# HGRN scores for four heads at once in shared tiles, with three runs of level products and another order of gates, queries and values

## The chip, the cores and the metric

The kernel runs on one core of a Trainium2 chip. A core has a matrix engine (TensorE, PE in the profile, with its weight loads as PEld), three engines for elementwise work (VectorE or DVE, ScalarE or ACT, GpSimd or POOL) and a sequencer, SyncE or SP, that issues most of the DMA. They run side by side, each through its own queue in order, and wait for each other through semaphores. The metric is the time of one execution on the device in microseconds. Three executions of the kernel before took 1251.87, 1251.75 and 1250.62 us, so the median is 1251.75.

## What is computed

The program is a decoder of four layers over 256 tokens of width 1024. Each layer is a token mixer and a SwiGLU feed-forward block, each followed by a residual and a layer norm. The mixers are HGRN2, mLSTM, S5 and HGRN2 again. The change touches HGRN alone, which therefore runs twice, as the first and as the last layer. Per head (eight heads, 128 wide) its reference is this, by chunks, with `s_prev` the state that one chunk hands to the next:

```python
q, f, v, g = jnp.split(x @ w_in, 4, axis=-1)
log_f = jnp.logaddexp(jnp.log(lb), jnp.log1p(-lb) + jax.nn.log_sigmoid(f))
k = (1.0 - lb) * jax.nn.sigmoid(-f)
q = jax.nn.silu(q)
...
b = jnp.cumsum(lfb, axis=2)
diff = b[:, :, :, None, :] - b[:, :, None, :, :]
decay = jnp.exp(jnp.where(mask[:, :, None], diff, -jnp.inf))
att = jnp.einsum('bhtd,bhsd,bhtsd->bhts', qb, kb, decay)
o = jnp.einsum('bhts,bhse->bhte', att, vb) + jnp.einsum('bhtd,bhde->bhte', qb * jnp.exp(b), s_prev)
...
o = _head_rmsnorm(_from_chunks(oc), norm_w) * silu(g)
```

So the score of token t for an earlier token s is the sum over 128 channels of q, k and the product of the forget gates between them. In the first HGRN layer the bound `lb` is zero; in the last one it is not, and the gates then need two more instructions per head.

## The kernel before

**Projections.** A matrix of float32 is kept as a rounded part `hi` and a rest `lo`, and a product is three matmuls (`mm3`, lines 182 to 184). A weight stage of 1 MB comes by DMA (`fetch`, line 110, issued by SP, three staging buffers), is rounded by ACT (`halve`, line 151) and its rest is made by DVE (line 152), 1024 columns at a time. The list made by `plan` gives the order of stages, and `wstage` emits the splitting of the next stage when a stage is taken. Values and output gates are projected token by token, 512 columns wide, by `pieces`, four pieces of 12 matmuls for half the heads. Queries and forget gates are projected transposed, for two heads at a time, by `pair_proj`: 48 matmuls of 256 columns.

**Gates.** `hgrn_gates` makes k and f of two heads from one projection, with three ACT instructions, two on DVE and two on ACT (`act` is line 95), and in the last layer four bound instructions more. They need one activation table, the Silus of the queries another; `table` loads a table (line 88) and orders the activations around it.

**Scores.** A product of gates over a range of tokens can be split at any token in the range, so the scores are built by levels. At level m (1, 2, 4, ... 64) the tokens stand in pairs of neighbouring blocks of m; the query rows of the one block have been multiplied by the gates up to the block's edge, the key rows of the other by the gates from there, and one small product gives the scores between the two. `hgrn_scores` does this for a pair of heads, as a generator that yields after each level. It makes the diagonal products (line 654), masked by DVE into the tile `near` (line 655). For each level below 32, ACT copies the keys into `kk` (line 664), PE makes eight products of 32 by 32 (line 668), and DVE puts the valid ones into `near` by `copy_predicated` (line 671). Levels 32 and 64 are line 677, and their results go to the score tile `att` by ACT (line 684), the diagonal blocks by DVE (line 680). After the products of a level DVE multiplies keys, queries and the block's gate products in place (line 640), which the next level needs. The last step is the product between the two halves of the sequence (line 700), copied to `cross`.

**Order.** `scores` walks two pairs of heads level by level, and between the levels emits other work: the remaining query projections and the values during the first two pairs, the output gates during the last two. The framework places each engine's instructions by a list schedule in which earlier program order has priority and a ready instruction can fill a gap; the order is then fixed. `heads_out` makes the products with the values and the head norm, `turn` the gating and the transposes into `ot`, and `out_proj` the output projection. PSUM, where PE writes, has four banks with the tag `a` (scores, queries), two with `g` (projections) and two with `t`.

## Time and profile before

| what | value |
|---|---|
| median of three runs | 1251.75 us |
| the profiled execution: its time | 1251.88 us |
| the profiled execution: its span | 1250.1 us |
| mean granted clock of TensorE | 0.997 |

The page of the profile gives for each engine the time in which one of its instructions ran, as a share of the span. A matmul is pipelined: its duration overlaps with the next one's, and what it costs its neighbours is read from the distance of the starts in the timeline. The rows of the timeline are: start, duration, engine, line, operation, output and inputs, shapes, count. A row that stands for several merged instructions gives the time from the start of the first to the end of the last. In the groups by line the figures after the bar are the busy time in us and the mean duration of one in ns, then the idle time ahead of them.

### The profile page before, as it was taken

What the parts mean: (1) busy time and instruction counts of PE and PEld (TensorE: products, weight loads), DVE (VectorE), ACT (ScalarE), POOL (GpSimd) and SP (SyncE); (2) the same over time, 40 slices, a digit from 0 to 9 for tenths busy, and PEclk for the clock granted to TensorE, in tenths of its full rate; (3) what the DMA queues carried; (4) which work ended last, traced back from release to release, by engine and by line L of the source; (5) the groups of instructions that cost most, each with busy time, mean ns of one, the idle gap of its engine ahead of it and who ended that gap; (6) DMA issues with size and microseconds to landing.
All of it is one profiled execution on the core that took longest, in us unless ns stands there. A gap on an engine that the chain in (4) does not pass through costs nothing.

```text
span 1250.1 us, 21400 instructions
## 1 busy us (share of the span) xinstructions
PE 1230.6 (98%) x8464; PEld 1031.6 (83%) x8464; DVE 956.2 (76%) x1717; ACT 694.3 (56%) x1126; POOL 34.8 (3%) x63
## 2 busy tenths in 40 slices
PE   9999999999999999999999999999999999999997
PEld 8977888888798888888877788888889878888886
DVE  6887889796887799887699696666486887766664
ACT  7755575565477555555544355555359654555551
POOL 0000000000100000000000000000000000000000
PEclk9999999999999999999999999999999999999999
DMA  8733476666373288667565456555446432755540
GB/s 325 290 137 135 150 267 236 219 220 225 121 274 129 102 305 307 234 235 247 209 217 210 165 202 231 191 181 201 169 173 219 157 134 102 270 184 186 194 143 34
DMA packets 50245, 247.91 MB, mean 198 GB/s; under 512 B 6337, under 2 KB 15953, under 8 KB 23777
## 3 DMA queue, kind: packets, MB, share of 16 engines
q1 hardware_dynamic: 50016, 246.46, 55.0%
q8 instruction: 66, 1.08, 0.3%
q14 instruction: 35, 0.28, 0.1%
q0 software_dynamic: 128, 0.09, 0.0%
HBM read 233.94 MB, written 12.58 MB: 197 GB/s over the span
## 4 chain that ended last, share of the span: by engine, by line
PE 88%; DVE 6%; DMA 2%; ACT 2%; issue 1%; POOL 0%; SPq 0%; DVEq 0%; ACTq 0%; POOLq 0%
PE g L212 18%; PE g L182 10%; PE g L184 10%; PE g L183 9%; PE g L215 9%; PE a L183 8%; PE a L182 8%; PE a L184 8%; DVE lo L152 2%; PE a L374 1%; PE t L273 1%; DMA bc<-in_s_bc 1%; PE a L668 1%; DMA w<-in_w_gu 1%; PE a L548 1%
## 5 line engine op out<-in xcount | busy, mean ns | idle before, releaser
L152 DVE TENSOR_TENSOR lo<-w,hi 128x1024 fp32r<-128x1024 f32 x388 | 470.3, 1219 | 117.6 <-ACT hi L151 107.6
L151 ACT CAST hi<-w 128x1024 fp32r<-128x1024 f32 x388 | 405.3, 1051 | 186.5 <-PE a L183 98.0
L212 PE MATMUL g<-xx,hi 128*128 128x512 f32 x1024 | 356.6, 397 | 0.5 <-DVE sum L356 0.4
L215 PE MATMUL g<-xx,lo 128*128 128x256 f32 x1024 | 264.6, 279 | 0.0
L212 PEld LDWEIGHTS g<-xx,hi 128*128 128x128 f32 x1024 | 185.8, 188 | 37.5 <-DVE sum L356 1.2
L215 PEld LDWEIGHTS g<-xx,lo 128*128 128x128 f32 x1024 | 193.0, 188 | 10.8
L182 PE MATMUL g<-hi,xx 128*128 128x512 f32 (+1 forms) x416 | 166.5, 401 | 2.4 <-ACT xx L292 2.1
L184 PE MATMUL g<-lo,xx 128*128 128x512 f32 (+1 forms) x416 | 163.7, 395 | 0.0
L183 PE MATMUL g<-hi,xx 128*128 128x512 f32 (+1 forms) x416 | 163.4, 394 | 0.0
L183 PE MATMUL a<-hi,hl 128*128 128x512 f32 x328 | 129.3, 394 | 1.0 <-DVE hl L345 1.0
L182 PE MATMUL a<-hi,hh 128*128 128x512 f32 x328 | 129.0, 394 | 0.1
L184 PE MATMUL a<-lo,hh 128*128 128x512 f32 x328 | 129.0, 393 | 0.0
L355 ACT COPY sum<-g 128x256 f32<-128x256 f32 x128 | 47.7, 373 | 139.7 <-PE g L212 139.5
L356 DVE TENSOR_TENSOR sum<-g,sum 128x256 f32<-128x256 f32 x128 | 53.9, 421 | 61.9 <-ACT sum L355 61.5
L182 PEld LDWEIGHTS g<-hi,xx 128*128 128x128 f32 x416 | 78.4, 189 | 19.3 <-ACT xx L292 3.5
L184 PEld LDWEIGHTS g<-lo,xx 128*128 128x128 f32 x416 | 78.2, 188 | 16.4 <-DVE lo L152 0.4
L183 PEld LDWEIGHTS g<-hi,xx 128*128 128x128 f32 x416 | 78.4, 188 | 14.6
L183 PEld LDWEIGHTS a<-hi,hl 128*128 128x128 f32 x328 | 61.6, 188 | 15.6 <-DVE hl L345 1.8
L184 PEld LDWEIGHTS a<-lo,hh 128*128 128x128 f32 x328 | 61.6, 188 | 13.6
L182 PEld LDWEIGHTS a<-hi,hh 128*128 128x128 f32 x328 | 61.5, 188 | 13.3 <-ACT hh L344 0.9
L182 PE MATMUL g<-xx,hi 128*128 128x256 f32 x192 | 54.5, 284 | 0.0
L184 PE MATMUL g<-xx,hi 128*128 128x256 f32 x192 | 54.4, 283 | 0.0
(308 smaller groups left out, 1734.9 us busy)
## 6 DMA issues: line engine op xcount, KB each, us to landing
w<-in_w_gu SPq DMA_DIRECT2D x88, 1024.0 KB
w<-in_w_dn SPq DMA_DIRECT2D x44, 1024.0 KB
w<-in_w_hg SPq DMA_DIRECT2D x30, 1024.0 KB
w<-in_w_ml SPq DMA_DIRECT2D x12, 1024.0 KB
gb<-in_ln SPq DMA_DIRECT2D x8, 1024.0 KB
w<-in_w_ho SPq DMA_DIRECT2D x8, 1024.0 KB
w<-in_w_so SPq DMA_DIRECT2D x8, 1024.0 KB
w<-in_w_mo SPq DMA_DIRECT2D x4, 1024.0 KB
```

The costliest lines, as they stand in the source:

```text
L151: self.nc.scalar.copy(hi, x)
L152: i = self.nc.vector.tensor_tensor(lo, x, hi.bitcast(F32), ALU.subtract).ins
L182: mm(ps, lh, rh, start=start, stop=False)
L183: mm(ps, ll, rh, start=False, stop=False)
L184: mm(ps, lh, rl, start=False, stop=stop)
L212: whole = lambda: mm(ps, hi[:, c], self.xx[:, k].rearrange("p i t -> p (i t)"), start=k == 0, stop=k == KD - 1)
L215: mm(ps[:, S:], lo[:, c], self.xh[:, k], start=False, stop=False)
L273: nc.tensor.transpose(pt[:, (k % 4) * P : (k % 4 + 1) * P], z[:, k * P : (k + 1) * P], self.ident)
L355: nc.scalar.copy(t, ps[:, S:])
L356: nc.vector.tensor_tensor(t, ps[:, 0:S], t, ALU.add)
L374: nc.tensor.matmul(down[h][n], hidden(h, j, b)[x], dn[j][b][y][:, f], start=False, stop=(x, y, b) == steps[-1])
L548: nc.tensor.matmul(o, att[:, 2 * h + hd % 2, :], v[:, h, c], start=True, stop=h == 0)
```

## The change

Queries, keys and gates of four heads now lie in one tile each, 1024 columns wide (`part`), and one walk of `hgrn_scores` does four heads, so that there are two walks per layer instead of four. At each of the six levels below 64, ACT copies keys and queries, as they stand, into saved tiles (`levels`), and DVE multiplies them for the next level at once. The products are made later: levels 1, 2 and 4 in one run, 8 and 16 in another, 32 and 64 in the last (`RUNS`). `order` holds every product of a run behind the run's first, which is taken from the last of its levels, so that a run is ready as a whole when it begins. The copies of the diagonal blocks go from DVE to ACT.

The order of the projections changes with it: gates 0 and 1, queries 0 and 1, then, after the first six levels in the program, gates 2 and 3 and queries 2 and 3, each group behind a table load of its own, then the values. The mask tile is larger and is loaded after the first two gates. One score tile instead of three serves all heads, `near`, `ends` and `cross` have one buffer each, and the two halves of `ot` share buffers with the first two level tiles.

```diff
 MASKED = (1, 2, 4, 8, 16)
+NEAR = MASKED + (32,)
 BIG = 1e30
 AHEAD = 1
 ROWS = (0, 1, NBLK - 1)
 GAPS = (32, 256, 448)
+RUNS = ((1, 2, 4), (8, 16), (32, 64))
 
 
...
-            msk = hp.tile([P, len(MASKED) + 1, 64], F32, name=self.uid("msk"))
-            atts = [hp.tile([P, 512], F32, name=self.uid("att")) for _ in range(3)]
-            for t in atts:
-                nc.gpsimd.memset(t, 0.0)
-            ot = self.transposed(hp)
+            msk = hp.tile([P, len(MASKED) * P + 80], F32, name=self.uid("msk"))
+            att = hp.tile([P, 1024], F32, name=self.uid("att"))
+            nc.gpsimd.memset(att, 0.0)
             v = hp.tile([P, 2, D], F32, name=self.uid("v"))
             g = hp.tile([P, 2, D], F32, name=self.uid("g"))
 
...
+
+            def part(n, name, pr):
+                if (n, name) not in quads:
+                    quads[n, name] = wp.tile([P, 1024], F32, tag=name, name=self.uid(name))
+                return quads[n, name].rearrange("p (h x) -> p h x", h=2)[:, :, pr % 2 * 256 : pr % 2 * 256 + 256]
...
+                return self.hgrn_scores(hp, wp, *(quads[n, x] for x in "qkf"), msk, att)
+
+            def walk(n, run, times=1):
+                for _ in range(times):
+                    mem[n] = next(run)
 
             for halves in (both,) if j == 0 else ((0,), (1,)):
                 block(v, AF.Copy, 0, 0, halves)
-            self.table("natural_log_exp_and_others")
-            for pr in range(4):
-                gates(pr)
-            nc.sync.dma_start(msk, self.a["c_lvl"])
+            exp, silu = "natural_log_exp_and_others", "silu_and_others"
+            self.table(exp)
+            gates(0)
+            gates(1)
+            nc.sync.dma_start(msk[:, 0 : len(MASKED) * P + 32], self.a["c_lvl"])
             nc.sync.dma_start(nw, self.a["hg_nw"][j])
-            self.table("silu_and_others")
+            self.table(silu)
             query(0)
             query(1)
             v1 = pieces(v, AF.Copy, 0, 1)
             g0, g1 = (pieces(g, AF.Silu, 12, n) for n in range(2))
-            scores((0, 1), ([], [lambda: query(2)], [], [lambda: query(3)], v1[0:1], v1[1:2], v1[2:3], v1[3:]))
-            late = []
-            scores((2, 3), ([lambda: late.append(heads_out(0))], g0[0:1], g0[1:2] + [lambda: late.pop()()], g0[2:3], g0[3:], g1[0:1], g1[1:2], g1[2:3]))
+            first = scores(0)
+            walk(0, first, len(NEAR))
+            self.table(exp)
+            gates(2)
+            gates(3)
+            self.table(silu)
+            query(2)
+            walk(0, first)
+            query(3)
+            v1[0]()
+            walk(0, first)
+            v1[1]()
+            second = scores(1)
+            walk(1, second)
+            v1[2]()
+            walk(0, first)
+            walk(1, second, len(NEAR) - 1)
+            v1[3]()
+            walk(0, first)
+            g0[0]()
+            late = heads_out(0)
+            g0[1]()
+            g0[2]()
+            late()
+            g0[3]()
+            walk(1, second)
+            g1[0]()
+            g1[1]()
+            walk(1, second)
+            g1[2]()
+            walk(1, second)
+            g1[3]()
+            walk(1, second)
             gb = gb()
-            g1[3]()
+            ot = tuple(hp.tile([P, KD, S], F32R, tag="o", name=self.uid(n), bufs=2) for n in ("oh", "ol"))
             for h in range(2):
                 turn(0, h)
             heads_out(1)()
             self.out_proj(("w_ho", j), gb, ot, lambda h: turn(1, h))
...
+    def hgrn_gates(self, wp, pr, pf, lb, k, f):
 
         nc, act = self.nc, self.act
-        k, f = (wp.tile([P, 512], F32, tag=t, name=self.uid(t), bufs=4) for t in "kf")
         l = wp.tile([P, 512], F32, tag="t", name=self.uid("t"))
         act(l, pf, AF.Abs)
         act(l, l, AF.Exp, scale=-1.0)
         act(l, l, AF.Ln, bias=1.0)
+        pf, l = (x.rearrange("p (h x) -> p h x", h=2) for x in (pf, l))
...
+    def hgrn_scores(self, hp, wp, q, k, f, msk, att):
...
+        queries = lambda t, m: view(t, m, (512 - m, 2), (2 * m, 256 // m), (1, m))
+        whose = lambda e, m, s: view(e, s, (512 // m + 1 - 2 * s, 2), (2, 256 // m), (0, m))
+        eight = lambda x: x.rearrange("p (a t) -> p a t", a=8)
+        heads = lambda x: x.rearrange("p (a t) -> p a t", a=4)
         rows = lambda c: slice(32 * c, 32 * c + 32)
+        near = wp.tile([P, 256], F32, tag="near", name=self.uid("near"), bufs=1)
+        levels = [hp.tile([P, 2048], F32, tag="o", name=self.uid("lev"), bufs=2) for _ in range(2)]
+        levels.append(wp.tile([P, 2048], F32, tag="lev", name=self.uid("lev"), bufs=1))
+        saved = [t[:, i * 512 : (i + 1) * 512] for t in levels for i in range(4)]
+        k8, q8, a8 = eight(k), eight(q), eight(att)
+        pd = self.bank("a")[:, 0:256]
+        lead = None
+        for i in (2, 3, 6, 7, 0, 1, 4, 5):
             for c in range(4):
+                mm = nc.tensor.matmul(pd[rows(c), rows(i)], k8[:, i, rows(c)], q8[:, i, rows(c)], start=True, stop=True).ins
+                self.order(mm, lead)
+                lead = lead or mm
+        nc.vector.tensor_tensor(eight(near), eight(pd), msk[:, None, len(MASKED) * P : len(MASKED) * P + 32].broadcast_to([P, 8, 32]), ALU.mult)
         mul(q, q, f)
+        e, ends = f, wp.tile([P, 512], F32, tag="ends", name=self.uid("ends"), bufs=1)
         spare = 0
+        for g, m in enumerate(NEAR):
+            n = 512 // m
+            kc, qc = saved[2 * g : 2 * g + 2]
+            nc.scalar.copy(view(kc, 0, (m, 2), (2 * m, 256 // m), (1, m)), keys(k, m))
+            nc.scalar.copy(view(qc, 0, (256, 2), (m, 256 // m), (1, m)), queries(q, m))
+            for x, y in ((keys(k, m), 1), (queries(q, m), 0)):
+                mul(x, x, whose(e, m, y))
+            new = ends[:, 0:n]
+            if m > 1:
+                new, spare = f[:, spare : spare + n], spare + n
+            mul(new, e[:, 0::2], e[:, 1::2])
+            e = new
+            yield
+        for run in RUNS:
+            pl, lead = self.bank("a"), None
+            at = dict(zip(run, (pl[:, i * P :] for i in range(len(run)))))
+            for m in run[::-1]:
+                kc, qc = saved[2 * NEAR.index(m) : 2 * NEAR.index(m) + 2] if m < 64 else (k8, q8)
+                for a in range(4):
                     for c in range(4):
+                        o, x = at[m][rows(c)], kc
+                        if m < 32:
+                            o = o[:, 0:P].rearrange("p (h a t) -> p a h t", h=2, a=4)[:, a]
+                            x, y = kc[:, a * P + 32 * c :][:, 0:32], view(qc, (4 * a + c) * 16, (256, 2), (1, 16))
+                        elif m == 32:
+                            o = o[:, rows(a)]
+                            x, y = kc[:, a * P + 32 * c :][:, 0:32], qc[:, c % 2 * 256 + (2 * a + c // 2) * 32 :][:, 0:32]
+                        else:
+                            h = c // 2
+                            o = o[:, a * 64 : a * 64 + 64]
+                            x, y = k8[:, 4 * h + a, rows(c)], q8[:, 4 * h + a, 64 * (1 - h) : 64 * (2 - h)]
+                        mm = nc.tensor.matmul(o, x, y, start=True, stop=True).ins
+                        self.order(mm, lead)
+                        lead = lead or mm
+            for m in run:
+                if m < 32:
+                    three = lambda x: x.rearrange("p (h b m) -> p h b m", h=2, m=m)
+                    g = MASKED.index(m)
+                    nc.vector.copy_predicated(view(near, m, (P - m, 2), (2 * m, 64 // m), (1, m)), three(i32(msk[:, g * P : (g + 1) * P])), three(at[m][:, 0:P]))
+                    continue
+                for c in range(4) if m == 32 else ():
+                    nc.scalar.copy(a8[rows(c), :, rows(c)], eight(near[rows(c)]))
                 for s in range(0, P, m):
                     h = s // m % 2
                     t = s + m * (1 - 2 * h)
+                    nc.scalar.copy(a8[s : s + m, 4 * h : 4 * h + 4, t : t + m], heads(at[m][s : s + m, 0 : 4 * m]))
             if m < 64:
+                yield
+        for x, h in ((k8, 0), (q8, 4)):
+            x = x[:, h : h + 4, 0:64]
+            mul(x, x, e.rearrange("p (a s) -> p a s", s=2)[:, h : h + 4, 1:].broadcast_to([P, 4, 64]))
+        yield
         pc = self.bank("a")
+        for a in range(4):
+            nc.tensor.matmul(pc[:, a * P : (a + 1) * P], k8[:, a], q8[:, 4 + a], start=True, stop=True)
+        cross = wp.tile([P, 4, P], F32, tag="cross", name=self.uid("cross"), bufs=1)
+        nc.scalar.copy(cross, heads(pc))
+        yield a8, cross
...
-            p += [("w_hg", j, s) for s in (0, 1, 8, 9, 10, 11, 4, 5, 6, 7, 2, 3, 12, 13, 14, 15)] + [("w_ho", j, s) for s in range(4)]
+            p += [("w_hg", j, s) for s in (0, 1, 8, 9, 4, 5, 10, 11, 6, 7, 2, 3, 12, 13, 14, 15)] + [("w_ho", j, s) for s in range(4)]
...
-        lvl.append(np.concatenate([same & ((s // m) % 2 == h) for h in (0, 0, 1, 1)], 1))
-    lvl.append(s % 32 == np.arange(64)[None, :])
+        lvl += [same & ((s // m) % 2 == h) for h in (0, 1) for _ in range(4)]
+    lvl.append(s % 32 == np.arange(32)[None, :])
```

83 lines of the change are left out of this document (12 added, 71 removed).

## The prediction

> **What bounds the kernel.** I read the page first: the busy shares, then the chain that ended last. (On the page, PEld is TensorE's weight load.)
>
> ```profile
> span 1250.1 us, 21400 instructions
> ...
> PE 1230.6 (98%) x8464; PEld 1031.6 (83%) x8464; DVE 956.2 (76%) x1717; ACT 694.3 (56%) x1126; POOL 34.8 (3%) x63
> ...
> PE 88%; DVE 6%; DMA 2%; ACT 2%; issue 1%; POOL 0%; SPq 0%; DVEq 0%; ACTq 0%; POOLq 0%
> ```
>
> TensorE (PE) is busy 98% of the span and is 88% of the chain. Next, the busy time by stage of the two HGRN layers: the projections of gates and first queries, then the scores, for the first layer and for the last one.
>
> ```profile
> 16.70:51.40 34.70, 34.70 (x290) 34.55 (x288) 25.92 (x28) 30.26 (x42) 0.00 (x0) 1.00 0.86 316
> 51.40:108.00 56.60, 56.48 (x834) 44.80 (x834) 49.53 (x141) 32.57 (x68) 2.62 (x2) 1.00 0.37 133
> 933.20:970.30 37.10, 37.10 (x296) 36.13 (x294) 22.14 (x24) 33.44 (x55) 0.00 (x0) 1.00 0.65 243
> 970.30:1024.00 53.70, 53.55 (x821) 42.42 (x821) 49.85 (x142) 31.96 (x68) 2.19 (x2) 1.00 0.33 120
> ```
>
> The columns are the length, then busy PE, PEld, DVE (VectorE), ACT (ScalarE), POOL, clock, DMA share and GB/s. PE has no idle time worth naming in any of the four. So time can be won here only by making PE's own sequence shorter. Busy time does not say how well PE is fed, so I looked at start times in PE's timeline, around a run of small score products.
>
> ```profile
> 55.66 0.39 PE L183 MATMUL g<-hi,xx 128*128 128x512 f32 x1
> 55.98 0.46 PE L668 MATMUL a<-q,kk 128*32 128x32 f32 x32
> 56.37 0.50 PE L184 MATMUL g<-lo,xx 128*128 128x512 f32 x1
> 56.71 0.39 PE L182 MATMUL g<-hi,xx 128*128 128x512 f32 x1
> 56.94 0.40 PE L183 MATMUL g<-hi,xx 128*128 128x512 f32 x1
> ...
> 72.94 0.33 PE L677 MATMUL a<-q,k 128*32 128x32 f32 x16
> 73.21 0.51 PE L182 MATMUL g<-hi,xx 128*128 128x512 f32 x1
> 73.64 0.33 PE L677 MATMUL a<-q,k 128*32 128x32 f32 x16
> ...
> 103.25 0.39 PE L184 MATMUL g<-lo,xx 128*128 128x512 f32 x1
> 103.57 0.65 PE L677 MATMUL a<-q,k 128*32 128x64 f32 x32
> 104.15 0.50 PE L182 MATMUL g<-hi,xx 128*128 128x512 f32 x1
> 104.49 0.40 PE L183 MATMUL g<-hi,xx 128*128 128x512 f32 x1
> ```
>
> Undisturbed, a 512-wide projection product starts 0.23 us after the one before (56.71 to 56.94). From 55.66 to 56.71 PE did two of them and one run of 32 records (each product of this type is two records): 1.05 - 0.46 = 0.59 us for the run. From 72.94 to 73.64 it did a run of 16 and one projection product: 0.70 - 0.23 = 0.47. So 16 records cost 0.12 us, 7.5 ns each, and **0.35 us is the price of interrupting** the projections, whatever the run holds: the wide product before ends late, the one after starts late and slow. A run of 32 records 64 wide costs 1.24 - 0.46 = 0.78, so 13.4 ns a record over the same 0.35.
>
> **What the change takes from PE.** The first score run of each layer and the last of layer 3; the last of the first layer is the row at 103.57 above:
>
> ```profile
> 51.42 0.46 PE L654 MATMUL a<-q,k 128*32 128x32 f32 x32
> ...
> 970.32 0.46 PE L654 MATMUL a<-q,k 128*32 128x32 f32 x32
> ...
> 1019.63 0.65 PE L677 MATMUL a<-q,k 128*32 128x64 f32 x32
> ```
>
> Between them I count 23 interruptions by L654, L668 and L677 in each layer (two adjacent runs as one). The new code has four runs for four heads: the diagonal products, levels 1, 2 and 4, levels 8 and 16, levels 32 and 64. That is 8 per layer. The number of small products stays; here it is for the first layer:
>
> ```profile
> L668 PE MATMUL a<-q,kk 128*32 128x32 f32 x320 | 5.6, 200 | 0.0
> L677 PE MATMUL a<-q,k 128*32 128x64 f32 (+1 forms) x128 | 2.6, 212 | 0.1
> L654 PE MATMUL a<-q,k 128*32 128x32 f32 x128 | 1.9, 198 | 0.0
> ```
>
> By the code half of L677 is 32 wide, so 512 records at 7.5 ns and 64 at 13.4 ns, 4.7 us. Before: 23 x 0.35 + 4.7 = 12.75 us. After: 8 x 0.35 + 4.7 = 7.5. That is 5.25 us per layer; two of the 23 stand beside the products with the values and shared a switch with them, so I take **5.0 per layer, 10.0 in all**. The crosswise product (L700) keeps its records and loses one or two cheap switches of about 0.1 us: nothing.
>
> One price is not in these rows. The new runs hold 64 to 96 records of the narrow kind; the longest above is 48. S5 has a long run, of the wider kind:
>
> ```profile
> 644.48 1.99 PE L1206 MATMUL g<-s5u,bm 128*32 128x64 f32 x128
> 646.40 0.39 PE L183 MATMUL a<-hi,xx 128*128 128x256 f32 x1
> ```
>
> 128 records in 1.92 us is 15 ns each with the switch, the pace of the short 64-wide run, so length itself slows nothing there. Whether PE is fed at 7.5 ns for that long is open. If past 32 records the pace fell to 13.4 ns, 32 + 64 + 32 + 32 = 160 records per four heads would lose 5.9 ns each: 0.9 us, 3.8 in the kernel. The lower end is 0; I take 0, since the form of these records is that of the 7.5 ns rows.
>
> **What it does to the other engines.** Prices, in the first layer's HGRN stretch, then two rows of the last layer, then the table load and its neighbours, and the issue of the mask:
>
> ```profile
> L152 DVE TENSOR_TENSOR lo<-w,hi 128x1024 fp32r<-128x1024 f32 x34 | 40.7, 1219 | 10.7 <-ACT hi L151 10.7
> L151 ACT CAST hi<-w 128x1024 fp32r<-128x1024 f32 x33 | 34.2, 1045 | 13.9 <-PE g L183 9.8 <-PE a L184 4.0
> L640 DVE TENSOR_TENSOR q<-q,f 128x256 f32<-128x256 f32 x20 | 8.4, 418 | 0.0
> L95 ACT ACTIVATE t<-t 128x512 f32<-128x512 f32 x8 | 5.0, 629 | 0.0
> ...
> 952.57 0.59 ACT L95 ACTIVATE f<-f,odds 128x256 f32<-128x256 f32 x1
> 953.06 0.50 ACT L95 ACTIVATE k<-k,odds 128x256 f32<-128x256 f32 x1
> ...
> 45.07 0.64 ACT L95 ACTIVATE k<-k 128x512 f32<-128x512 f32 x1
> 45.72 1.28 ACT L88 ACT_TABLE_LOAD   x1
> 47.02 0.60 ACT L95 ACTIVATE q<-a 128x512 f32<-128x512 f32 x1
> ...
> msk<-in_c_lvl SPq DMA_DIRECT2D x2, 192.0 KB
> ```
>
> DVE gets lighter: for four heads two instructions 256 wide (2 x 0.42 us) become one 512 wide (about 0.68: the rows of 256 and 1024 elements lie 801 ns and 768 elements apart, 1.04 ns an element). For the 24 such pairs per layer that is 0.16 each, 4 us, and the copies of the diagonal go to ACT. ACT gets heavier: per four heads and level one 512-wide copy of keys and one of queries (0.63 each by L95) where there were two copies of keys, and two more table loads per layer, 2.6 us.
>
> The crowded place is new. Gates 2 and 3 and queries 2 and 3 now run on PE while the first six levels are multiplied. PE has four projections of 48 products there, at 34.70 / 290 = 0.12 us each: 23.0 us. ACT must do four weight splits (8 x 1.05), two gate pairs (10 x 0.63), twelve level copies (12 x 0.63), two table loads and three Silus (0.6 each): 26.6 us. The last layer adds eight bound instructions, 4 x 0.59 + 4 x 0.50 = 4.4, so 31.0. If nothing could be moved, PE would lack 3.6 and 8.0 us, 11.6 together. But much can move. In the two query projections before it, ACT has per projection of 5.8 us only a split and a Silu (2.7), so about 6 us of splits can be made ahead, as far as buffers allow; the last gate pair's exponentials and the Silus may run late, since the second four heads start only after 24 products of the values, 24 x 0.23 = 5.5 us later. The row 933.20:970.30 shows how this ends: ACT 90% busy and PE still without a gap. The bounds are 0 and 11.6.
>
> A second crowded place is the six levels of the second four heads, which must be done before PE has used up the rest of the values and the output gates. From their start to their last run PE has 24 + 48 + 36 projection products, 24.8 us, and some 7 us of runs and of products with the values. DVE needs there twelve level products (8.2), about 5 for the other instructions of the levels and for masks, ten splits (12.2) and 2.7 at the heads' output, 28 of 32 us. That share is the one of the row 51.40:108.00, 49.53 of 56.60, where PE did not wait; if it fails, PE stands idle late in the layer. For both places together I take 1.5 us, near the two rows without a gap.
>
> The Trainium skill speaks against the extra loads: "ScalarE: Activation LUTs", section "What ACT_TABLE_LOAD costs", puts a switch at about 2.66 us, 1.28 of load and 1.38 of drain, and asks to group by set. Here the load took 1.28 us, began where the activation at 45.07 ended and was followed 0.02 us later: the drain does not show. By the page's figure ACT would carry 5.5 us more over the kernel, an estimate, and the sum would stay as it is while ACT is off PE's path.
>
> Smaller edits, at nothing. The mask tile grows from 192 KB to 336 KB and its DMA moves ahead of gates 2 and 3 on SP's queue; the weight fetches behind it come 144 KB / 316 GB/s = 0.5 us later, three staging buffers ahead of use. The masked diagonal tile has one buffer, so the second four heads' diagonal product on DVE must wait for ACT's copies after the first four's last run, one piece of values (12 x 0.23 = 2.8 us) and the run of about 1 us later; behind it on DVE stand level products and a split, while PE has two pieces prepared, 5.5 us. The output halves share buffers with the level copies; they are needed some 10 us after the last reader.
>
> **Sum.** The profiled execution took 1251.9 us for its span of 1250.1; the median of the runs is 1251.75, 0.1 less. 1251.75 - 10.0 + 1.5 = **1243.2**.
>
> **Rivals.** (1) The work cannot be moved so far and PE waits 4 to 7 us in the crowded places of both layers: 1245.7 to 1248.7. For: 26.6 and 31.0 against 23.0. Against: the slack just named. Nothing measurable is left if the waits reach 7.5 to 12.5 us: about 1251. (2) **Slower**: the level copies and products, earlier in the program, sit ahead of the weight splits on ACT's and DVE's queues. A level alone is two copies and two products, 2 x 0.63 + 2 x 0.68 = 2.6 us if ACT and DVE alternate without overlap, 15.7 for six; one stage prepared ahead feeds PE for 5.8, so PE stands for 10 us per layer, 20 in all: 1262. It decides from 5 us per layer. For: the twelve copies and twelve products are one chain through both engines. Against, the queues of before in the first levels:
>
> ```profile
> 52.02 1.05 ACT L151 CAST hi<-w 128x1024 fp32r<-128x1024 f32 x1
> ...
> 53.10 1.23 DVE L152 TENSOR_TENSOR lo<-w,hi 128x1024 fp32r<-128x1024 f32 x1
> ```
>
> Splits were placed between the level steps. (3) It does not do what it says: projections slip into the runs, or long runs lose pace. Half the interruptions kept leaves 1247; the lost pace gives 1246.5. One page bears on the pace: "TensorE: Matmul & The Clock Gate" of the Trainium skill, in its table of figures, gives a queue 64 deep, less than a run of 96 with its weight loads. The S5 run, twice that, kept pace, so it has little weight.
>
> **Chances.** Forecast with PE waits under 4 us 56% (1241 to 1245.7), rival 1 as a gain 14%, rival 3 7%, waits that eat the gain 11%, slower 12%. The range of 1240.2 to 1250.5 leaves out rival 2, the upper part of the eaten gain, and below it a few per cent. 0.2% is 2.5 us, about what a measurement of this kernel tells from no change. Faster 0.77, same 0.11, slower 0.12.
>
> **What would show it.** Right: in each HGRN layer PE's timeline has eight runs of 64 or more small records instead of 23, a 96-record run with its switch takes about 1.07 us (0.35 + 96 x 7.5 ns), and the first projection product of query 3 starts no later than 23 us after that of gate 2 plus the runs between. Wrong: idle time before weight loads, released by L151 or L152, between gates 2 and the second block of values, or before the last runs of a layer; runs at 13 ns a record; or small runs split by projection products.

## The result and the profile after

The changed kernel took 1242.92 us (median; 1242.01 to 1243.72), the kernel before 1251.66 us beside it: a ratio of 0.9932, 95% interval 0.9917 to 0.9947. In a second comparison, further below, it took 1243.04 against 1250.28, ratio 0.9939 (0.9927 to 0.9951). The ratios compare executions at full clock: one of the five executions with the values by VectorE, in the experiments below, took 2006.62 us at a granted clock of 0.556 and is left out. The profiled execution took 1242.15 us. Its page has these lines in the place of those shown of before:

```profile
span 1240.4 us, 21170 instructions
...
PE 1220.3 (98%) x8464; PEld 1029.4 (83%) x8464; DVE 943.3 (76%) x1577; ACT 713.8 (58%) x1126; POOL 32.5 (3%) x59
...
PE 85%; ACT 6%; DVE 6%; DMA 2%; issue 1%; SPq 0%; DVEq 0%; POOL 0%; ACTq 0%
```

TensorE has the same 8464 matmul records and is as full as before, and its busy time fell by 10.3 us. To see where, cut both executions at the same four places: the first gate projection of each HGRN layer, and the last product with values of that layer. Here are busy times by stretch, before and then after (length first, then PE, PEld, DVE, ACT, POOL, clock, DMA share, GB/s): first HGRN layer, everything between the two, last HGRN layer.

```profile
16.78:116.85 100.07, 99.95 (x1177) 87.12 (x1176) 81.76 (x175) 68.34 (x119) 2.62 (x2) 1.00 0.57 208
116.85:933.22 816.37, 805.78 (x5013) 671.78 (x5012) 644.29 (x1151) 445.49 (x707) 23.89 (x45) 1.00 0.58 207
933.22:1032.91 99.69, 99.55 (x1171) 86.44 (x1170) 77.76 (x171) 70.97 (x131) 2.19 (x2) 1.00 0.48 177
```

```profile
17.38:113.37 95.99, 95.60 (x1177) 86.98 (x1176) 74.85 (x105) 77.60 (x119) 1.87 (x2) 1.00 0.59 217
113.37:927.24 813.87, 804.13 (x5012) 670.72 (x5011) 644.40 (x1151) 446.06 (x707) 23.26 (x43) 1.00 0.58 208
927.24:1023.17 95.93, 94.90 (x1172) 86.28 (x1170) 71.42 (x101) 80.61 (x131) 1.84 (x2) 1.00 0.51 181
```

The two HGRN layers are shorter by 4.08 and 3.76 us, 7.8 together. The spans differ by 9.7, because the stretch between the layers, which the change does not touch, was by chance 2.5 us shorter in this execution, while the start was 0.6 later. Most of the 2.5 is one place in S5. PE's timeline there, before and then after:

```profile
692.27 0.50 PE L183 MATMUL a<-hi,xx 128*128 128x512 f32 x1 [2.00 <-ACT xx L95]
...
693.00 0.63 PE L182 MATMUL a<-hi,xx 128*128 128x512 f32 x1
693.42 0.63 PE L183 MATMUL a<-hi,xx 128*128 128x512 f32 x1
```

```profile
688.90 0.50 PE L185 MATMUL a<-hi,xx 128*128 128x512 f32 x1 [2.08 <-ACT xx L97]
...
689.47 0.40 PE L184 MATMUL a<-hi,xx 128*128 128x512 f32 x1
689.70 0.40 PE L185 MATMUL a<-hi,xx 128*128 128x512 f32 x1
```

Both executions idle about 2 us there. In the one, products then start 0.43 us apart at a granted clock of 0.5; in the other 0.23 apart at 1.0. From the first of these rows to the next other work is 4.07 us in the one and 2.52 in the other, so 1.55 of the difference is this. A second profiled execution of the changed kernel had the dip again, and its span was 1242.9; its two layers were 7.2 us shorter than before. So the change itself is worth 7 to 8 us, 7.8 in the first execution. The ratios say 8.5 (0.0068 x 1251.66) and 7.6 (0.0061 x 1250.28), and the interval of each holds both layer figures.

Inside the layer, PE's timeline has the runs that the code asks for:

```profile
58.52 0.28 PE L186 MATMUL a<-xx,hi 128*128 128x256 f32 x1
58.73 1.03 PE L722 MATMUL a<-lev 128*32 128x32 f32 x96
59.69 0.39 PE L184 MATMUL a<-xx,hi 128*128 128x256 f32 x1
59.91 0.28 PE L185 MATMUL a<-xx,lo 128*128 128x256 f32 x1
...
68.39 0.76 PE L722 MATMUL a<-lev 128*32 128x32 f32 x64
69.08 0.50 PE L184 MATMUL g<-hi,xx 128*128 128x512 f32 x1
...
72.04 0.76 PE L684 MATMUL a<-q,k 128*32 128x32 f32 x64
75.66 0.65 PE L722 MATMUL a<-q,k 128*32 128x64 f32 x32
76.13 0.50 PE L722 MATMUL a<-lev 128*32 128x32 f32 x32
```

Two 256-wide products take 0.24 us when nothing is between them, so the run of 96 cost 59.91 - 58.52 - 0.24 = 1.15 us. By the sum of start distances over all eight runs and the products behind them, runs and switches together got some 4.8 us cheaper in each layer (from 12.9 and 13.1 to 8.2). 4.8 x 2 = 9.6, and 7.8 came out: some 1.8 us went into new waits and what came with them. The longest, in the last layer, on PE's timeline, and then ScalarE's (ACT) timeline at the same time:

```profile
988.63 1.05 PE L745 MATMUL a<-q,k 128*128 128x128 f32 x8
990.26 0.50 PE L184 MATMUL g<-hi,xx 128*128 128x512 f32 x1 [0.57 <-ACT v L527]
991.76 0.61 PE L548 MATMUL a<-v,att 128*128 128x128 f32 x4
992.73 0.50 PE L184 MATMUL g<-hi,xx 128*128 128x512 f32 x1 [0.37 <-ACT v L527]
```

```profile
986.48 1.89 ACT L736 COPY att<-a 32x128 f32<-32x128 f32 x6
988.39 0.67 ACT L695 COPY lev<-q 128x512 f32<-128x512 f32 x1
988.97 0.61 ACT L694 COPY lev<-k 128x512 f32<-128x512 f32 x1
989.61 0.60 ACT L527 ACTIVATE v<-g 128x512 f32<-128x512 f32 x1
```

The values are finished on PE when the crosswise product starts at 988.63, but ACT copies them out of PSUM at 989.61, behind score copies and level copies of the next four heads. PE needs the bank for the output gates and waits. The products with the values (L548) also fall into two pieces around this wait.

### The profile page after: what moved, and what is told of

Its sections match the earlier page's. It is cut to its first block, busy times and chain, and to the rows that moved or that the text cites. A ratio compares the mean times of both kernels' runs of the same rounds, so it can differ in the third digit from the quotient of the medians.

```text
span 1240.4 us, 21170 instructions
## 1 busy us (share of the span) xinstructions
PE 1220.3 (98%) x8464; PEld 1029.4 (83%) x8464; DVE 943.3 (76%) x1577; ACT 713.8 (58%) x1126; POOL 32.5 (3%) x59
## 4 chain that ended last, share of the span: by engine, by line
PE 85%; ACT 6%; DVE 6%; DMA 2%; issue 1%; SPq 0%; DVEq 0%; POOL 0%; ACTq 0%
PE g L214 18%; PE g L184 9%; PE g L217 9%; PE g L186 9%; PE g L185 9%; PE a L185 8%; PE a L186 8%; PE a L184 8%; ACT hi L153 2%; DVE lo L154 1%; PE a L376 1%; PE t L275 1%; DMA bc<-in_s_bc 1%; ACT L90 1%; DVE s5rot L1267 1%
## 5 line engine op out<-in xcount | busy, mean ns | idle before, releaser
L154 DVE TENSOR_TENSOR lo<-w,hi 128x1024 fp32r<-128x1024 f32 x388 | 470.8, 1220 | 119.5 <-ACT hi L153 110.7
L153 ACT CAST hi<-w 128x1024 fp32r<-128x1024 f32 x388 | 404.9, 1051 | 173.1 <-PE a L185 96.2
L217 PE MATMUL g<-xx,lo 128*128 128x256 f32 x1024 | 264.6, 279 | 0.0
L186 PE MATMUL g<-xx,hi 128*128 128x256 f32 x192 | 54.5, 284 | 0.0
L185 PE MATMUL g<-xx,lo 128*128 128x256 f32 x192 | 54.4, 283 | 0.0
```

Of the source, the lines that this page charges most:

```text
L153: self.nc.scalar.copy(hi, x)
L154: i = self.nc.vector.tensor_tensor(lo, x, hi.bitcast(F32), ALU.subtract).ins
L185: mm(ps, ll, rh, start=False, stop=False)
L186: mm(ps, lh, rl, start=False, stop=stop)
L217: mm(ps[:, S:], lo[:, c], self.xh[:, k], start=False, stop=False)
```

## The experiments

All of them are one edit of the changed kernel, except the one on order, which is an edit of the kernel before. The theory (A) is that of the prediction: PE's sequence is made of projections, narrow runs and a price per interruption. The stretch is the length of an HGRN layer, cut as above; the groups are the narrow runs per HGRN layer that PE's timeline shows.

| kernel | groups | stretch, first | stretch, last | ratio to before (95%) |
|---|---|---|---|---|
| before | 23 | 100.07 | 99.69 | 1 |
| order alone | 20 | 98.69 | 98.25 | 0.9975 (0.9963 to 0.9988) |
| seven runs | 14 | 97.67 | 97.26 | 0.9972 (0.9962 to 0.9982) |
| changed | 8 | 95.99 | 95.93 | 0.9932 (0.9917 to 0.9947) |
| changed, again | 8 | 95.97 | 96.56 | 0.9939 (0.9927 to 0.9951) |
| values by VectorE | 8 | 95.02 | 94.94 | 0.9922 (0.9909 to 0.9934) |
| values first | 8 | 95.46 | 95.31 | 0.9935 (0.9913 to 0.9958) |
| two runs | 6 | 98.76 | 99.34 | 1.0014 (1.0005 to 1.0022) |
| two runs, relieved | 6 | 96.46 | 96.04 | 0.9965 (0.9953 to 0.9978) |
| joined runs | 3 | 99.05 | 101.88 | 1.0008 (0.9997 to 1.0018) |

**Order alone.** The kernel before, two heads at a time, with gates 2 and 3 put between the first levels and the order of queries and values of the change:

```diff
-            for pr in range(4):
+            for pr in range(2):
                 gates(pr)
...
-            scores((0, 1), ([], [lambda: query(2)], [], [lambda: query(3)], v1[0:1], v1[1:2], v1[2:3], v1[3:]))
+            scores((0, 1), ([lambda: self.table(exp), lambda: gates(2)], [lambda: gates(3), lambda: self.table(silu)], [lambda: query(2)], [lambda: query(3)], v1[0:1], v1[1:2], v1[2:3], v1[3:]))
```

> The kernel before with the new order of projections alone: gates 0 and 1, queries 0 and 1, then gates 2 and 3 and queries 2 and 3 between the levels of the first two pairs, with the two further table loads; scores in pairs, level by level, as before. TensorE's program has 20 interruptions by small products in each HGRN layer instead of 23, since some of them now fall together. Theory A: 3 x 0.35 = 1.05 us less per layer, about 1249.6 us, up to 1252 if TensorE waits in the crowded place. Theory B (the order carries the gain): near 1243 us.

It took 1247.76 us, more of a gain than A had and far from B. The layers got 1.38 and 1.44 us shorter, where three interruptions fewer account for 1.05 each; what the other 0.35 is was not followed. So the order carries about a third of the change's 7.8, and, by the price of an interruption, most of that by having fewer of them.

**Seven runs.** Four heads at once as in the change, but one run per level, with a step of the walk after each projection or piece:

```diff
-RUNS = ((1, 2, 4), (8, 16), (32, 64))
+RUNS = ((1,), (2,), (4,), (8,), (16,), (32,), (64,))
...
             gates(2)
+            walk(0, first)
             gates(3)
+            walk(0, first)
...
```

> The changed kernel, with the six levels and level 64 sent as seven runs between products instead of three; tiles shared by four heads, saved copies and the order of projections stay. In each HGRN layer TensorE's program has 14 interruptions by small score products instead of 8. Theory A (an interruption costs 0.35 us, whatever it holds): 6 x 0.35 = 2.1 us more per layer, 4.2 in all, about 1247.1 us. Theory B (the gain came from lighter VectorE work, the saved copies and the new order, the number of runs does not matter): 1242.9 us, and HGRN stretches as long as in the changed kernel, 96.0 us.

1247.32 us: A. The layers are 1.68 and 1.33 us longer than in the changed kernel. Six interruptions at 0.35 would be 2.1. The trace shows what is lacking. Around one of the runs of 32 records PE starts its products at 69.51, 70.21 and 70.55 us, so the run costs 1.04 - 2 x 0.23 = 0.58; the run of 96 in the changed kernel cost 1.15. Three short runs in place of that one are 0.60 more, 0.30 for each further interruption, because the records of a short run go by faster (about 7 ns each, 8.4 in the runs of 64 and 96). In the last layer, PE also idles 0.60 us in all, against 0.95 in the changed kernel.

**More cuts.** The price itself, by adding interruptions: in the middle of each piece of the second values block and of the output gates stands one more narrow product, which nobody reads.

```diff
-                    self.as_part(dict(enumerate(ps)), [us[u]], 2 * u)
+                    self.as_part({0: ps[0]}, [us[u]], 2 * u)
...
+                    cut = nc.tensor.matmul(spare[0][0:32, 0:32], self.ident[:, 0:32], self.ident[:, 0:32], start=True, stop=True).ins
+                    self.order(cut, self.last)
+                    self.as_part({1: ps[1]}, [us[u]], 2 * u)
```

> The changed kernel with 12 more products per HGRN layer, each 32 rows by 32 columns of the identity, put singly between two 512-wide projection products in the middle of a piece of the values or output gates; their results are read by nobody. 24 more interruptions in all. A (each interruption of the projections costs 0.35 us, and about 8 ns per record): 24 x (0.35 + 0.02) = 8.8 us more, 1242.9 + 8.8 = 1251.7, and each HGRN layer's stretch 4.4 us longer than 96.0. B (what the change gained was the waits around the old order of work, and a single narrow product between two wide ones costs its own 8 to 25 ns): under 1 us, 1243 to 1244.

1250.82 us against 1250.02 for before: ratio 1.0002 (0.9992 to 1.0012). Twenty-four products of two records each eat the gain of the whole change. PE's timeline around one of them, then from the view of that one source line PE's idle time ahead of it (the sum, and how often):

```profile
66.86 0.39 PE L186 MATMUL g<-lo,xx 128*128 128x512 f32 x1
67.18 0.25 PE L526 MATMUL t<-ident 128*32 128x32 f32 x2
67.36 0.50 PE L184 MATMUL g<-hi,xx 128*128 128x512 f32 x1
67.69 0.39 PE L185 MATMUL g<-hi,xx 128*128 128x512 f32 x1
```

```profile
  issue: 8.6, 24
```

From 66.86 to 67.69 PE starts two wide products and the narrow one: 0.83 - 2 x 0.23 = 0.37 us. By the stretches, 4.12 and 4.33 us longer with 12 more products each, it is 0.34 and 0.36. The idle ahead of each is 8.6 / 24 = 0.36, and nothing that the profile shows ends it. This is A's number, and B (a single narrow product costs its own few nanoseconds) falls.

**Wide cuts.** The same, with the whole identity as the weights:

```diff
-                    cut = nc.tensor.matmul(spare[0][0:32, 0:32], self.ident[:, 0:32], self.ident[:, 0:32], start=True, stop=True).ins
+                    cut = nc.tensor.matmul(spare[0][:, 0:32], self.ident[:, :], self.ident[:, 0:32], start=True, stop=True).ins
```

> As the run with 24 more 32 by 32 products, but each added product uses all 128 rows and all 128 columns of the identity as its weights, with 32 moving columns, and writes all 128 partitions. A1 (the price is that of going from the whole array to a 32-column part of it and back): these cost no more than the crosswise products' switches did, about 0.1 us and 0.1 us for the records, so 24 x 0.1 to 0.2 = 2.4 to 4.8 us, 1245.3 to 1247.7. A2 (the price belongs to going from the products of halves to plain fp32 products, whatever the shape): as much as with the 32 by 32 products, 8.8 us, about 1251.7.

1247.45 us, ratio 0.9975 (0.9966 to 0.9985). PE's timeline:

```profile
66.30 0.39 PE L186 MATMUL g<-lo,xx 128*128 128x512 f32 x1
66.53 0.30 PE L526 MATMUL t<-ident 128*128 128x32 f32 x2
66.67 0.48 PE L184 MATMUL g<-hi,xx 128*128 128x512 f32 x1
66.98 0.40 PE L185 MATMUL g<-hi,xx 128*128 128x512 f32 x1
```

Now the cost is 66.98 - 66.30 - 0.46 = 0.22 us, 0.14 of it the two records, and the product starts on time, 0.23 after the one before. By the stretches it is (98.50 - 95.99) / 12 = 0.21. The time lies at the upper end of A1's range and far from A2: such a product costs a little more than A1 had, and the delay ahead of it is gone. That delay belongs to the 32-column form. "TensorEngine Tiling (Array Packing)" in the Trainium skill, section "Key Properties", says that a change of tiling mode drains TensorE; the rows agree, and put the price of going there and back at 0.37 us with one product in it.

**Two runs.** Levels 1 to 8 in one run of 128 records, 16 to 64 in one of 96:

```diff
-RUNS = ((1, 2, 4), (8, 16), (32, 64))
+RUNS = ((1, 2, 4, 8), (16, 32, 64))
...
             query(2)
-            walk(0, first)
             query(3)
...
             g1[1]()
-            walk(1, second)
             g1[2]()
```

> Levels 1, 2, 4 and 8 in one run of 128 records and 16, 32 and 64 in another of 96, each set of four heads with its diagonal apart as in the changed kernel, so 6 interruptions per HGRN layer instead of 8. A (price of an interruption 0.35 us, runs of up to 128 records hold no idle, since a block of TensorE's instructions is 128 records long and no run uses up two of them): 2 x 2 x 0.35 = 1.4 us less than the changed kernel, 1241.5 or a ratio of 0.992, HGRN stretches about 95.3. F2 (a run of 128 records already uses up its block before the next has landed): an idle of 0.5 to 3 us without a releaser in at least one run, 1243 to 1248. W (the levels' copies are late for the longer runs): idle of 1 us or more in the products around them with ScalarE or VectorE as releaser, 1242 to 1245.

1252.96 us, ratio 1.0014 (1.0005 to 1.0022): W, and worse than W gave. The runs hold no idle, the waits come behind them. PE's timeline in the first layer, then ACT's:

```profile
79.20 1.05 PE L743 MATMUL a<-q,k 128*128 128x128 f32 x8
81.86 1.35 PE L548 MATMUL a<-v,att 128*128 128x128 f32 x10 [1.60 <-issue]
```

```profile
78.57 1.68 ACT L730 COPY att<-near 32x256 f32<-32x256 f32 x4
80.27 1.88 ACT L734 COPY att<-a 32x128 f32<-32x128 f32 x6
```

PE is through with the crosswise products at 80.26 and starts the products with the values at 81.86, when the score copies (L734), which they read, are nearly through. The trace names no releaser for this wait; that it is these copies is read from the times. With all later levels in one run, all their copies come at once and last, on an engine that is full. The two layers are 6.2 us longer than in the changed kernel and what follows the last one is 1.3 longer; the rest of the 10 us lies in the layers between and was not followed.

**Joined runs.** As the two runs, but the runs moved until a run stands directly behind another and the second heads' diagonal behind that, so that there are only three groups per layer:

```diff
+            walk(0, first, 2)
             second = scores(1)
             walk(1, second)
...
-            walk(1, second)
             g1[0]()
             g1[1]()
-            walk(1, second)
+            walk(1, second, 2)
             g1[2]()
```

> The changed kernel with all seven levels of four heads sent in one go, from two banks of results, the first one joined to the diagonal products of the second four heads: 3 interruptions by small products in each HGRN layer instead of 8. Theory A: 5 x 0.35 = 1.75 us less per layer, 3.5 in all, about 1239.4 us, if nothing new has to be waited for; the last scores are one piece earlier than before, so the masks and copies behind them have 5.5 us of products to hide in. Theory B: no gain, 1243 us or more.

1251.86 us: no gain, as B had it, and 9 us lost besides, which neither theory gave. The gain of five interruptions is more than lost again, and by idle time inside the groups, for which the trace has no releaser. PE's timeline in the last layer, then busy time by stretch, then the DMA queues in the first two of these stretches (packets, MB, share):

```profile
985.22 0.56 PE L680 MATMUL a<-q,k 128*32 128x32 f32 x40
990.76 0.54 PE L680 MATMUL a<-q,k 128*32 128x32 f32 x22 [4.98 <-issue]
```

```profile
986.00:988.40 2.40, 0.00 (x0) 0.00 (x0) 1.89 (x7) 0.00 (x0) 0.00 (x0) 1.00 0.99 406
988.40:989.40 1.00, 0.00 (x0) 0.00 (x0) 0.00 (x0) 0.00 (x0) 0.00 (x0) 0.95 1.12 401
991.00:995.00 4.00, 4.00 (x30) 3.17 (x21) 3.20 (x6) 2.24 (x6) 0.00 (x0) 0.50 0.05 18
```

```profile
q1 hardware_dynamic: 131, 0.97, 99.0%
...
q1 hardware_dynamic: 51, 0.39, 105.7%
q8 instruction: 1, 0.02, 5.8%
```

PE stops in the middle of 64 like products; 42 of them are done, and from 987.92 on no engine does anything. Only the DMA engines are full, with weights, until at 988.4 one packet of another queue comes through: q8, instructions. PE goes on 1.4 us after it has landed, at half clock (0.50 in the last of the three stretches), which costs more.

The page says what q8 is. These are its rows of the changed kernel and, ahead of its description, of the long runs below:

```profile
q8 instruction: 66, 1.08, 0.3%
```

```profile
q8 instruction: 74, 1.21, 0.4%
```

8464 matmuls and as many weight loads, 16928 instructions, in 66 packets: 256 a packet. The long runs add 2 x 1024 instructions and have eight packets more, again 256 each. So q8 brings PE's instructions, 128 records with their loads at a time. At 8.4 ns a record a block is used up in 1.1 us; in projections it lasts 15 us or more. A new theory (F), then: a narrow run that uses up a whole block before the next has landed stops PE.

**Long runs and short runs.** To test F without data to wait for: 128 products of the identity (256 records) in a row, at two places of each HGRN layer; and the same products 32 at a time, in each of eight pieces.

```diff
+                    add, lead = 128 if (st, n, u) in ((0, 1, 2), (12, 0, 2)) else 0, self.last
+                    for i in range(add):
...
+                        c = i % 4 * 32
+                        cut = nc.tensor.matmul(spare[0][c : c + 32, 0:32], self.ident[:, 0:32], self.ident[:, 0:32], start=True, stop=True).ins
+                        self.order(cut, lead)
+                        lead = cut if i == 0 else lead
```

The short runs have `32 if (st, n) in ((0, 1), (12, 0)) else 0` in the first line.

> The changed kernel with two runs of 128 more narrow products (256 records each) per HGRN layer, one in the middle of the third piece of the values and one in the middle of the third piece of the first output gates; operands are the identity, there since the start, and results are read by nobody. By the price of an interruption and the pace, each run costs 0.35 + 256 x 8.4 ns = 2.5 us, 10.0 us in all. F (TensorE's instructions come in blocks of 16 KB, 128 records with their weight loads each, by DMAs that queue behind the weights; in a run of over 128 records at 8.4 ns TensorE uses them up faster than they come): each run holds an idle of 1 to 5 us with no releaser, ended by the landing of such a block, 4 x 2.5 = 10 us more, about 1263 (1257 to 1270). D (the idle in the joined runs was a wait for the levels' copies): no idle, since nothing is waited for, 1252.9.

> The same 2 x 128 more narrow products per HGRN layer as in the long runs, but 32 products (64 records) in the middle of each of the four pieces of the values and of the first output gates. By the price of an interruption: 16 x 0.35 + 1024 x 8.4 ns = 14.2 us more than the changed kernel, about 1257.1 under F and D alike, with no idle in the runs; so slower than the long runs by 4.2 us under D, faster by some 6 under F.

Long runs 1265.43 us, ratio 1.0119 (1.0104 to 1.0134); short runs 1257.55 us, ratio 1.0053 (1.0036 to 1.007). F gave 1263 and 1257.1, D the reverse order. One of the long runs in PE's timeline:

```profile
74.22 1.06 PE L529 MATMUL t<-ident 128*32 128x32 f32 x101
75.95 1.28 PE L529 MATMUL t<-ident 128*32 128x32 f32 x128 [0.67 <-issue]
79.68 0.64 PE L529 MATMUL t<-ident 128*32 128x32 f32 x27 [2.44 <-issue]
```

The middle piece is 128 records, one block exactly. The packets of q8 in the trace show what ends the stops (us):

```
kernel         PE stops  packet starts   landed  PE goes on  after landing
long runs         75.28          73.24    74.39       75.95           1.56
long runs         77.23          77.05    78.28       79.68           1.40
long runs        100.25          99.98   100.94      102.34           1.40
long runs        997.31         998.03   998.99     1000.23           1.24
long runs       1004.72        1002.76  1003.70     1005.06           1.36
long runs       1020.61        1018.63  1019.69     1021.07           1.38
joined runs       72.03          71.54    72.71       73.97           1.26
joined runs      103.70         103.52   104.48      105.75           1.27
joined runs      985.78         988.42   989.35      990.76           1.41
short runs        74.75          73.15    74.03       75.58           1.55
```

These are all the stops of 0.3 us or more within the narrow runs of the three kernels, and every time PE goes on 1.24 to 1.56 us after the landing. Counted in PE's records, the stops of one layer lie 128 and 383 apart in the first layer of the long runs, 128 and 255 in the last, and 383 in the first layer of the joined runs: multiples of 128, to one record. The waits behind the two runs above are of another kind, for there the last packet had landed 2.9 and 2.8 us before PE went on.

The short runs' expectation of no idle missed once, at 74.75, though the 128 records ahead of that stop took 4.7 us. Of the blocks of 128 that PE went through in 1.2 to 1.5 us, seven out of eight ended in a stop; the other three stops came behind blocks of 2.9 to 4.7 us. So it is not the length of one run that counts, nor the pace alone, but whether the next packet has landed when a block ends; what decides when a packet is sent was not followed. "Runtime: NRT & Kernel Launch" in the Trainium skill, section "Instruction fetch mechanics", has the stream come in blocks of 16 KiB, 256 instructions, and takes the fetch to be mostly hidden; the packets agree, and the stops show where it is not hidden. The changed kernel has none of these stops in its HGRN layers, where 128 records never pass in less than some 4 us. With a run of 96 go 32 products of 0.12 us, 96 x 8.4 ns + 3.8 = 4.6 us; with two runs of 64 the twelve products of 0.23 between them, 116 x 8.4 ns + 2.8 + 0.35 = 4.1. It has one in S5, which the change does not touch: in the first profiled execution the second run of 128 records there stops for 0.62 us and goes on 1.40 us after a packet's landing.

**Values first.** The wait behind the crosswise product came from ACT's queue. Here the last piece of the values stands ahead of the second heads' levels in the program:

```diff
-            walk(1, second, len(NEAR) - 1)
             v1[3]()
+            walk(1, second, len(NEAR) - 1)
```

> The changed kernel with the last piece of the values ahead of levels 2 to 32 of the second four heads in the program, so that ScalarE copies the values out of their two banks before the level copies; nothing else moves on TensorE. Theory A (TensorE waits there for these copies: 0.17 and 0.26 us and a split group of products with the values in the first layer, 0.74 and 0.25 in the last, about 1.7 us in all with the extra switches): 1.7 us less, 1241.2 us, the HGRN stretches 95.3 and 94.9 us. Rival (ScalarE is full in that place, so the wait moves to the levels): no gain, 1242.9 us.

1242.58 us, ratio 0.9935 (0.9913 to 0.9958). The layers are 0.53 and 0.62 us shorter and the products with the values are in one piece again, so the reading holds, with 1.15 of the 1.7 us; in the whole time it cannot be seen.

**Values by VectorE.** The direct test: the two copies of the second values block made by VectorE (DVE).

```diff
-                        f = nc.scalar.activation if func == AF.Copy else self.act
                         for h in range(2):
-                            f(dst[:, h, n * 512 : (n + 1) * 512], ps[h], func)
+                            o = dst[:, h, n * 512 : (n + 1) * 512]
+                            if func == AF.Copy:
+                                nc.vector.tensor_copy(o, ps[h])
+                            else:
+                                self.act(o, ps[h], func)
```

> The changed kernel with the two copies of the second values block out of PSUM made by VectorE instead of ScalarE, in both HGRN layers. S (the waits of TensorE behind the crosswise products and the first products with values come from these copies standing in ScalarE's queue behind level and score copies and weight splits): they shrink by 0.3 to 0.8 us a layer, stretches 95.4 and 95.2, 1241.5 to 1242.5. V (VectorE is as full there with level products and the low halves of the weights, so the copies come no sooner): waits as long or longer with VectorE as releaser, 1243 to 1245.

Ratio 0.9922 (0.9909 to 0.9934), the profiled execution 1239.65 us, the lowest here. Busy time by stretch, both layers:

```profile
16.89:111.91 95.02, 95.02 (x1178) 86.84 (x1176) 75.72 (x107) 76.70 (x117) 2.23 (x2) 1.00 0.60 219
925.71:1020.65 94.94, 94.63 (x1172) 86.06 (x1170) 72.31 (x103) 79.67 (x129) 2.14 (x2) 1.00 0.51 185
```

The layers are 0.97 and 0.99 us shorter than in the changed kernel, more than S gave: in the first PE has no idle at all. That is 1.96 us for a copy on the wrong engine, 1.1 of it idle that the trace of the changed kernel shows as waits for this copy; the rest lies around the products with the values, which are in one piece again. The ratio is better than the changed kernel's in both comparisons, though the intervals overlap.

**Two runs, relieved.** The two runs again, with this copy by VectorE and the products with the values one piece later:

```diff
+            g0[1]()
             late = heads_out(0)
-            g0[1]()
```

> The two longer runs per set of heads again, with the two copies of the second values block made by VectorE, and the products with the values of the first four heads one piece of the output gates later. If what the two longer runs lost were the waits of TensorE for score copies and values behind ScalarE's queue, and nothing in the runs themselves: 6 interruptions instead of 8 at 0.35 us, 1.4 us less than the changed kernel with its values copied by VectorE, HGRN stretches about 94.3, ratio about 0.991. If the copies are late for these runs wherever the products stand: waits of 1 us or more in a layer remain, stretches 95.5 or longer, ratio 0.993 or more.

> The changed kernel itself, beside the two longer runs relieved: ratio 0.993, as before.

1245.43 us, ratio 0.9965 (0.9953 to 0.9978), beside 0.9939 for the changed kernel in the same comparison. More than half of what the two runs had lost came back; which of the two edits did more was not separated. But waits remain, as the second reading had it: 0.6 us in each layer for ScalarE's copy of the crosswise product, 0.5 in the last one for the values, and 1.3 behind its stretch for the heads' output on VectorE. There is also one stop of 0.4 us in a run. Of the numbers of groups tried here, eight is the best.

## Why the prediction was right, and where it was off

The forecast of 1243.2 us came out as 1242.92 and 1243.04.

- **PE bounds the kernel, and only a shorter sequence of its own helps.** Right: PE kept 98%, and its busy time fell with the span.
- **0.35 us per interruption.** Right and the core of it: 0.36 us of idle ahead of each added narrow product, 0.37 by start distances. From before to the kernel with the values by VectorE, 15 interruptions fewer made 5.05 and 4.75 us, 0.34 and 0.32 each. Between the seven runs and the changed kernel it was about 0.3, since longer runs go a little slower.
- **23 to 8, 10.0 us in all.** Nearly: the runs and switches gave some 9.6, from 12.9 and 13.1 to 8.2 where the prediction had 12.75 and 7.5. The term that was off is the pace: 64 records took 0.69 us to the next start and 96 took 0.96, so 8.4 ns a record, not 7.5, and the run of 96 cost 1.15 and not 1.07.
- **1.5 us of waits.** Near in size, 1.96 by the experiment that removed them, wrong in cause. The first crowded place, gates and queries under the first levels, has no wait of note in the first execution; in the second one PE stands 0.6 us ahead of the last layer's first diagonal product, for the Silu of the queries behind a table load. The second place has them, but not for weight splits (L153 and L154, as the prediction said to look for): the release of the PSUM banks by ACT's copy of the values was late. Rival 1's mechanism is this one, at a price below its 4 us.
- **Slower, by levels queued ahead of the splits.** Did not come: in the HGRN layers of the changed kernel PE waits nowhere for a split.
- **The run of 96 keeps its pace.** Nearly: 8.4 ns a record, far from the 13.4 of the rival. The prediction took length to be harmless by the S5 run of 128, which goes at 15 ns a record. That reading was too narrow: the second such run of S5 stops for 0.25 us in the kernel before too, and goes on 1.43 us after a packet of instructions has landed. In runs of 256 narrow records the stops are up to 2.9 us. The prediction did not have the supply of instructions; that the change kept clear of it in its own layers was luck.
- **The sum.** With 7.8 us for the two layers the profiled execution would have ended at 1244.1 and not at 1242.2; the rest was the clock dip in S5 and other chance outside the change. So the hit to 0.3 us is luckier than the terms, which are off by some 0.4 and 0.5.

## What to carry to other kernels

Count the times that a matmul stream is interrupted by products of another form, and read the price of one from start distances: here about 0.35 us, whether the run holds 2 records or 96, on an engine that shows 98% busy either way. Join the runs until what they need or release falls due all at once, and then look at which engine empties PSUM. Keep a burst of small matmuls below the number that one block of instructions holds, or put long ones between.

## What was not expected of the hardware

- TensorE's instructions arrive by DMA in blocks of 256, and PE waits where the next block has not landed: 0.3 to 5.0 us a stop, with no releaser in the trace. It did so behind seven of the eight blocks whose 128 records passed in 1.2 to 1.5 us, and longest while the weights filled the DMA engines (0.99 of them busy in the stop of 5.0).
- An idle of about 2 us on PE can halve the clock for the products behind it: idles of 2.00 and 2.13 us (before, two runs) did, idles of 2.05 and 2.08 (joined runs, changed) did not. The traces show part of the reason. Every such dip lasts 3.41 us or twice that and begins a whole multiple of 3.41 us after the clock's first rise. The first two idles lie within one such step; of the other two at most 1.54 and 1.19 us do. The limit is not sharp, for 1.50 us in one step halved the clock once (values first) and 1.94 left it alone once (joined runs). With the dip ten products took 1.55 us longer. Executions of one kernel differ by 1.7 us (the changed kernel) and more, and this is one reason that the traces show.
- A narrow product between wide ones costs 0.37 us in the 32-column form and 0.22 with all columns, and only the first starts late.
